# A convolution's very last half-image store as 120 partitions, with the other 8 in small pieces on one to seven DMA engines each

## The chip, the cores and the metric

One NeuronCore of a Trainium2 chip runs the whole program. The metric is device time of one execution in microseconds, the median of several executions, lower is better. A difference of under 2% counts as "same". TensorE, VectorE, ScalarE and GpSimd compute; SyncE issues the stores; 16 DMA engines move the data.

## The reference

A 3x3 convolution with padding 1 over 16 images of 64 channels and 64x64 pixels, to 128 output channels, in float32. Nine tenths of the weights are zero, but the kernel computes densely.

```python
batch, c_in, h, w, c_out, k = 16, 64, 64, 64, 128, 3
x_pad = np.pad(x, ((0, 0), (0, 0), (pad, pad), (pad, pad)))
# for every b, co, ci, kh, kw with weight != 0:
output[b, co] += weight[co, ci, kh, kw] * x_pad[b, ci, kh:kh+h, kw:kw+w]
```

One output image is 128 channels (partitions) x 64 rows x 64 columns x 4 bytes, 2 MB. All 16 are 33.55 MB.

## The kernel before

Images are computed in pairs. Each finished image is stored with one DMA; for the last pair the store is cut into two halves of 32 rows, so that less is left when compute ends. This loop is all that the change touches:

```python
    for p in range(NP):
        o = [o_pool.tile([C_OUT, H, W], FP32, name="o") for _ in range(2)]
        last = p == NP - 1
        for blk in range(4):
            r0 = 16 * blk
            # ... compute 16 rows of both images into o[0], o[1] ...
            if last and blk % 2 == 1:
                for n in range(2):
                    rows = slice(r0 - 16, r0 + 16)
                    nc.sync.dma_start(out=out[2 * p + n][:, rows, :], in_=o[n][:, rows, :])
        if not last:
            for n in range(2):
                nc.sync.dma_start(out=out[2 * p + n], in_=o[n])
```

The framework gives each DMA issued by SyncE one of eight completion semaphores, in rotation. A store that gets a semaphore first waits until that semaphore's previous user has landed. This is not visible in the code above.

## Time and profile before

| | kernel before |
|---|---|
| median (three runs) | 127.65 us |
| span of the profiled execution | 125.4 us |
| end of compute | 111.76 us |
| last packet of 15 DMA engines / of the sixteenth | 122.48 / 123.74 us |
| last arrival at the last store's semaphore | 124.20 us |

A store counts as landed when all its DMA engines have each added one to its semaphore; I call these additions **arrivals**. A 128-partition store has 16. The arrivals and the DMA packets are in the trace's own records, and tables of them are shown here in plain fences. The four half-image stores were issued by SyncE as follows (duration of an issue: smallest, median, largest):

```profile
L185 SPq DMA_DIRECT2D out_dram<-o x4: 332/417/612, 104.7 to 111.8; - x4
...
DMA to landing us min/median/max: 10.6/12.3/14.0
```

An issue takes a third to two thirds of a microsecond, and the data land ten or more later: there is a queue.

### The profile page before, as it was taken

The numbers are of one execution on the slowest core, as the hardware profiler recorded it, in microseconds if no ns is written. First come the engines' busy times: TensorE is split into PE (matmuls) and PEld (weight loads), VectorE is DVE, ScalarE is ACT, GpSimd is POOL, SyncE is SP. The second block draws the span as 40 slices with busy tenths as digits, with TensorE's granted clock in tenths as the row PEclk, the third lists the DMA queues.
The fourth block names the chain that finished last, engine by engine and source line by source line (L and its number), as shares of the span: only waits on it lengthen the run. The fifth ranks groups of instructions, "written<-read, shape, count | busy, mean of one in ns | idle before, by whom it ended". The sixth has DMA issues, their size and how long they took to land.

```text
span 125.4 us, 2486 instructions
## 1 busy us (share of the span) xinstructions
PE 107.5 (86%) x1002; PEld 58.8 (47%) x1002; DVE 82.4 (66%) x135; ACT 39.0 (31%) x71; POOL 40.7 (32%) x45
## 2 busy tenths in 40 slices
PE   6679999999999999999999999999999999920000
PEld 6435555555555555555555555555555555500000
DVE  0463877877787778777877787778777877760000
ACT  4555323333333333333333333333333333300000
POOL 6936533333333333333333333333333300000000
PEclk9999999999999999999999999999999999997555
DMA  5999999989999999999999999999999999999980
GB/s 146 338 222 220 212 214 220 191 259 350 324 311 337 308 293 319 342 316 308 426 429 423 408 429 434 450 416 434 418 418 429 429 444 423 434 397 423 423 369 10
DMA packets 4044, 42.93 MB, mean 342 GB/s; under 512 B 448, under 2 KB 448, under 8 KB 704
## 3 DMA queue, kind: packets, MB, share of 16 engines
q1 hardware_dynamic: 2880, 34.90, 66.2%
q0 software_dynamic: 1152, 7.86, 30.7%
q8 instruction: 8, 0.13, 0.4%
q14 instruction: 4, 0.03, 0.1%
HBM read 17.07 MB, written 33.55 MB: 404 GB/s over the span
## 4 chain that ended last, share of the span: by engine, by line
PE 81%; DMA 4%; DVE 1%; issue 1%; DVEq 0%; SPq 0%
PE ps L135 81%; DMA o<-in_x_dram 4%; DVE o L168 1%; DVEq L214 0%; DVE x L87 0%; SPq L60 0%; DVEq L168 0%
## 5 line engine op out<-in xcount | busy, mean ns | idle before, releaser
L168 DVE TENSOR_TENSOR o<-ps,pc 128x512 f32<-128x512 f32 x124 | 77.8, 686 | 22.1 <-PE ps L135 19.8
L135 PE MATMUL ps<-x,wT 64*128 64x504 bf16 (+3 forms) x780 | 88.8, 373 | 1.5 <-DVE x L87 1.5
L135 PEld LDWEIGHTS <-wT 64*128 64x128 bf16 x966 | 55.2, 94 | 49.4 <-issue 1.5
L154 POOL TENSOR_TENSOR s<-x 128x512 bf16<-128x512 bf16 x31 | 35.6, 1152 | 57.7 <-PE ps L135 41.5
L161 ACT COPY pc<-ps 128x512 f32<-128x512 f32 x62 | 33.3, 589 | 64.0 <-issue 61.8
L135 PE MATMUL ps<-s,wT 64*128 64x512 bf16 (+1 forms) x186 | 25.7, 377 | 0.0
L74 PE MATMUL ps<-idle_rhs 128*128 128x128 bf16 x27 | 3.1, 310 | 1.0 <-DVE idle_rhs L71 1.0
L67 POOL DMA_DIRECT2D x<-in_x_dram x7 | 3.7, 561 | 0.0
L74 PEld LDWEIGHTS <-idle_rhs 128*128 128x128 bf16 x27 | 2.8, 144 | 1.0 <-DVE idle_rhs L71 1.0
L91 DVE CAST w_bf<-w_sb 128x192 bf16<-128x192 f32 (+1 forms) x4 | 1.3, 382 | 3.0 <-DMA w_sb<-in_weight_dram 3.0
L149 DVE COPY o<-ps 128x512 f32<-128x512 f32 x2 | 1.4, 692 | 2.0 <-PE ps L135 2.0
L148 ACT COPY o<-ps 128x512 f32<-128x512 f32 x2 | 1.2, 586 | 2.4 <-PE ps L135 2.4
L87 ACT CAST x<-o 128x576 bf16<-128x576 f32 (+1 forms) x2 | 1.5, 802 | 0.5 <-DMA o<-in_x_dram 0.5
L91 ACT ACT_TABLE_LOAD x1 | 1.3, 1283 | 0.7 <-PEq L203 0.7
L97 PE MATMUL ps<-ident,w_bf 128*128 128x128 bf16 x9 | 1.1, 292 | 0.4 <-DVE w_bf L91 0.4
L87 DVE CAST x<-o 128x576 bf16<-128x576 f32 x1 | 0.5, 460 | 1.4 <-DMA o<-in_x_dram 1.4
L91 ACT CAST w_bf<-w_sb 128x64 bf16<-128x64 f32 (+1 forms) x2 | 0.7, 418 | 1.9 <-DMA w_sb<-in_weight_dram 1.9
L97 PEld LDWEIGHTS <-w_bf 128*128 128x128 bf16 x9 | 0.8, 128 | 0.8 <-DVE w_bf L91 0.8
L101 DVE TENSOR_TENSOR wT<-ps,wT 128x384 bf16<-128x384 f32 x2 | 1.0, 550 | 0.0
L63 POOL DMA_DIRECT2D x<-in_x_dram x1 | 0.7, 696 | 0.8 <-POOLq L203 0.8
L71 DVE MEMSET idle_rhs<- 128x64 uint32 x1 | 0.1, 112 | 0.8 <-PEq L203 0.8
L110 ACT CAST wT<-ps 128x384 bf16<-128x384 f32 x1 | 0.5, 481 | 0.4 <-PE ps L97 0.4
(8 smaller groups left out, 1.9 us busy)
## 6 DMA issues: line engine op xcount, KB each, us to landing
out_dram<-o SPq DMA_DIRECT2D x14, 2048.0 KB, 19.8
x<-in_x_dram POOLq DMA_DIRECT2D x7, 1024.0 KB, 29.3
out_dram<-o SPq DMA_DIRECT2D x4, 1024.0 KB, 12.3
o<-in_x_dram SPq DMA_DIRECT2D x1, 1024.0 KB, 5.4
x<-in_x_dram POOLq DMA_DIRECT2D x1, 512.0 KB, 7.5
w_sb<-in_weight_dram SPq DMA_DIRECT2D x1, 288.0 KB, 3.1
```

The source lines that it names most:

```text
L67: nc.gpsimd.dma_start(out=xs[p], in_=pair(p))
L74: nc.tensor.matmul(idle_ps, idle_rhs, idle_rhs, start=True, stop=True)
L87: copy(out=xs[0][:, a:b, :], in_=x_head[:, a:b, :])
L91: copy(out=w_bf4[:, g, a:b, :], in_=w_v[:, k : k + b - a, :])
L97: nc.tensor.matmul(wps[:, j, :], src, ident, start=True, stop=True)
L101: nc.vector.tensor_tensor(out=wT[:, g], in0=wps, in1=wT[:, G1], op=SUB)
L135: nc.tensor.matmul(ps[n][:, lo:hi, c_lo:c_hi], tap(g, kw, n), src[q, a:b:step, c_lo + kw - 1 : c_hi + kw - 1], start=(i == 0), stop=(i == ...
L148: nc.scalar.copy(out=o[0][:, r0 : r0 + rows, :], in_=ps[0])
L149: nc.vector.tensor_copy(out=o[1][:, r0 : r0 + rows, :], in_=ps[1])
L154: nc.gpsimd.tensor_tensor(out=s, in0=xs[p][:, r0 : r0 + 16 : 2, :], in1=xs[p][:, r0 + 1 : r0 + 16 : 2, :], op=ADD)
L161: nc.scalar.copy(out=c, in_=shared[n])
L168: nc.vector.tensor_tensor(out=o[n][:, first : r0 + 16 : 2, :], in0=ps[n], in1=pc[n], op=ADD)
```

## The change

The idea is that a whole DMA engine is spared in the last store. A copy of 120 partitions uses 15 engines, so the sixteenth has nothing more to do after the third half-store. The missing 8 partitions are stored as small pieces of 1, 7, 2, 6, 3, 5, 4 and 4 partitions by 8 rows, which run on as many engines as they have partitions, in a staircase over engines 0 to 6. If the spared engine were the one that is always last, the end would come earlier.

```diff
                 for n in range(2):
-                    rows = slice(r0 - 16, r0 + 16)
-                    nc.sync.dma_start(out=out[2 * p + n][:, rows, :], in_=o[n][:, rows, :])
+                    pieces = [(0, 128, r0 - 16, r0 + 16)]
+                    if (blk, n) == (3, 1):
+                        pieces = [(0, 120, r0 - 16, r0 + 16)]
+                        for i in range(4):
+                            r = r0 - 16 + 8 * i
+                            pieces += [(120, 121 + i, r, r + 8), (121 + i, 128, r, r + 8)]
+                    for c0, c1, a, b in pieces:
+                        nc.sync.dma_start(
+                            out=out[2 * p + n][c0:c1, a:b, :], in_=o[n][c0:c1, a:b, :]
+                        )
```

## The prediction

> **What bounds the kernel now.** I read the page's slices first, for the engines busy at the end, then the chain of waits, then the DMA issues with SyncE's own waits, and last the tail in short stretches.
>
> The 40 slices (3.13 us each):
>
> ```profile
> PE   6679999999999999999999999999999999920000
> DVE  0463877877787778777877787778777877760000
> ...
> DMA  5999999989999999999999999999999999999980
> ```
>
> TensorE and VectorE are done in slice 36 (about 112 us), while the DMA engines stay full for three more slices. So the last 13 us are a queue of stores being emptied; compute does not set the end.
>
> The chain that ended last says something else:
>
> ```profile
> PE 81%; DMA 4%; DVE 1%; issue 1%; DVEq 0%; SPq 0%
> ```
>
> These shares add up to 87 to 88%. In order of time, the chain's last piece is an addition that ends at 111.76 us; the view does not follow the stores after it. The remaining 13.6 us are therefore read elsewhere, here the DMA issues (count, size, median time to landing) and SyncE's waits:
>
> ```profile
> out_dram<-o SPq DMA_DIRECT2D x14, 2048.0 KB, 19.8
> out_dram<-o SPq DMA_DIRECT2D x4, 1024.0 KB, 12.3
> ```
>
> ```profile
> SPq L214 <- DMA out_dram<-o: 11.6, 4, 4.4
> ```
>
> A half-image store needs 12.3 us to land although its packets need far less: it queues behind earlier stores. At the end SyncE waits 11.6 us for the last four of them. The tail in stretches (PE alone; the columns after PE are granted clock, DMA share, GB/s):
>
> ```profile
> 121.50:122.00 0.50, 0.00 (x0) 0.50 0.70 295
> 122.00:122.50 0.50, 0.00 (x0) 0.50 0.16 66
> ```
>
> ```profile
> 122.50:123.70 1.20, 0.00 (x0) 0.00 (x0) 0.00 (x0) 0.00 (x0) 0.00 (x0) 0.50 0.06 27
> ```
>
> From 122.5 to 123.7 us the DMA share is 0.06, which is 1/16: one engine alone still has packets. The packet records of the trace say the same: 15 engines end their last packet between 120.93 and 122.48 us, one ends at 123.74. In the semaphore records the last store's 16 arrivals run from 121.28 to 122.84, with the sixteenth at 124.20. That engine, **the straggler**, is 1.36 us late. Its lag grew during compute: from 62.5 to 110.9 us one engine's 16 KB packets took 634 to 662 ns, where the others took 611; after 112 us all 8 KB packets take 309 ns. From the last arrival to the end of the span is 125.36 - 124.20 = 1.16 us of closing barrier.
>
> **What the Trainium skill says.** All four places are in the page "DMA: Bandwidth & Descriptors".
> - "Why a DMA increments its semaphore by 16 and not by 1": the number of DMA engines of a copy is the largest one up to 16 that divides the slowest dimension, and SyncE's copies use the lowest-numbered ones. So 120 partitions use engines 0 to 14, and the pieces of 7, 2, 6, 3, 5, 4, 4 partitions use as many engines from 0 up. The trace before has only 128-partition copies, with 16 arrivals each; it does not test the rest.
> - "Latency and other measured facts": engines 7 and 15 are usually slower. The trace agrees that one engine is, but does not number its packets. The page's guess is contention from GpSimd-issued transfers; here the slow packets come after the last of those (landed at 62.78), so the guess does not fit.
> - "Queues, rings and completion order": one engine takes its descriptors in ring order, and the semaphore increment lands only after that engine's earlier writes. So pieces queued behind the 120-partition store do not delay its arrivals.
> - "Anatomy of one DMA": about 2.0 us fixed per copy, mostly the write's confirmation. The trace differs in size: the weight load is issued at 0.74 and has its first packet at 1.75 (1.01 us), and a last semaphore packet lands 0.31 (weight load) to 0.46 us (straggler) later.
>
> **The change part by part.**
> 1. Removed: the 16th engine's share of the last store, 8 packets x 309 ns = 2.47 us. If engine 15 is the straggler, it now ends at 123.74 - 2.47 = 121.27, below the second-latest engine at 122.48.
> 2. Added: 32 rows of 2 KB on engines 0 to 6, namely 8, 7, 6, 5, 3, 2, 1. A 2304-byte packet of the weight load took 93 ns, so 2 KB is about 83 ns (estimate); engine 0 gets 8 x (83 + 9 for the semaphore packet) = 0.74 us. Without further waits the end would lie between the old second-latest 122.48 and 122.48 + 0.74: a gain of 0.5 to 1.3 us. That is the intent, at most 1%.
> 3. Added: eight issues on SyncE. The four last stores' issue records last 332 to 612 ns; eight such are 2.7 to 4.9 us after 112.4, against a backlog lasting until 122. Hidden.
> 4. **Moved into the path: semaphores.** The order of SyncE's instructions, built from the changed kernel, shows the stores rotating over eight completion semaphores, each new store waiting for that semaphore's previous user. With nine stores in place of one, the last rotation is short. Previous users by the trace of before: pieces 1, 2, 3: landed 99.16, 104.30, 109.45, no wait. Piece 4: landed 114.42. Piece 5: 116.87. Piece 6: 119.32. Piece 7: the third half-store, 121.77. **Piece 8 waits for the 120-partition store itself.** The first seven waits end under the backlog. The eighth cannot: it starts a full small-DMA latency after the end of the very transfer that used to be the end.
>
> Sum, straggler = engine 15: the 120-partition store lands on engines 0 to 14 at 122.84, the old second-latest arrival. Then 0.05 (wait to issue, a guess) + 1.01 (issue to first packet) + 0.15 (a 2 KB packet starting on an idle engine; the weight load's first ones took 91 to 346 ns) + 0.01 (semaphore packet) + 0.40 (to landing) = 1.62, so 124.46. With 1.16 for the barrier the span is 125.62, against 125.36: +0.26 us. The gain of 1.36 us and the new serial step of 1.62 us nearly cancel. On the timed median: 127.65 + 0.26 = 127.91; I say 127.9.
>
> **The rivals.**
> - The wait doesn't bite, and the straggler's relief is kept: 0.5 to 1.3 us gained, 126.4 to 127.1. For it: the backlog hides everything up to piece 7. Against: piece 8's wait is in the built order, and its target is the last large transfer. I give it 8%.
> - The straggler is among engines 0 to 14. Then nothing is relieved, piece 8 starts after 124.20, and 1.62 us come on top: 129.3. For it: the page names 7 as well, and no record numbers the engine. Against: the change is built around leaving out the last one. 20%.
> - Issue to first packet is longer than at the start. For it: the first output store was issued at 21.60 and its first packet ran at 25.76, 4.2 us later, though beside a queue of loads. Against: at 122.9 us the engines are idle and the queue has been running. If it took 2 us more, 129.9; 6%.
> - The timed runs had a larger lag than the profiled one (127.12 us against 127.65): a straggler later by 0.5 us would be relieved by that much more, giving about 127.4, as long as piece 7, which still waits for engine 15, is issued in time.
>
> **Range and chances.** The main case gives 127.5 to 128.4, from 0.3 us either way in the latency terms and 0.5 us in the lag. The rival with another straggler pulls the upper end to 129.4; the rival with no wait is left mostly outside. Range 127.1 to 129.4. Faster by 2% would need -2.55 us, and the whole relief is 1.36: 0.01. Slower by 2% needs +2.55, which only the long issue latency or several unlucky terms together reach: 0.04.
>
> **What would show it right or wrong.** In SyncE's records of the changed kernel the issues of pieces 4 to 7 should stand at about 114.4, 116.9, 119.3 and 121.8, and the eighth right after the last arrival of the 120-partition store, near 122.9. That store should have 15 arrivals ending near 122.84; if they end near 124.2, the straggler is not engine 15. The tail should have a gap of about 1 us with next to no packets, then four 2 KB packets, and the span should end about 1.6 + 1.2 us after that store's last arrival. If the eighth issue stands before 118 us, my reading of the semaphores is wrong and the gain should be there. If compute ends at another time than 111.8 us, something else moved.

## The result, and the profile after

The changed kernel takes 129.42 us (129.37 to 129.81, four runs), the kernel before on the same occasion 127.69. The ratio is 1.0139, with a 95% interval of 1.0116 to 1.0162. The kernel is clearly slower, and 129.42 lies just above the predicted range.

SyncE's own waits in the changed kernel:

```profile
SPq L192 <- DMA out_dram<-o: 2.6, 2, 2.2
SPq L223 <- DMA out_dram<-o: 0.7, 1, 0.7
```

Line 192 is the store loop: pieces now wait for other stores' landing, which no half-image store before had to do noticeably. The final wait for the stores (line 223) is down to 0.7 us from 11.6, because SyncE spends that time issuing and waiting inside the loop. Its issues:

```profile
L192 SPq DMA_DIRECT2D out_dram<-o x12: 252/1007/2078, 106.5 to 125.1; - x12
```

The last of them stands at 125.1 us, 11.5 us after the end of compute. The tail in stretches (granted clock, DMA share and GB/s are the last three columns):

```profile
123.80:124.60 0.80, 0.00 (x0) 0.50 0.05 20
125.00:125.70 0.70, 0.00 (x0) 0.50 0.00 0
125.80:126.20 0.40, 0.00 (x0) 0.50 0.07 21
126.20:127.60 1.40, 0.00 (x0) 0.50 0.00 0
```

Around 124 us one engine works alone, as before. Then nothing moves, and from 125.80 the four packets of the eighth piece follow. The arrivals (us) show what each step waited for:

```
store                issue    arrivals, last ones          late ones
third half-store     112.99   ... 120.86 121.09            122.54
120 partitions       113.59   ... 123.57 123.62            125.05
1 partition          114.75   121.79                       -
7 partitions         115.86   ... 123.58 123.67            125.24
2 partitions         116.91   122.15 123.75                -
6 partitions         118.00   ... 123.50 123.92            125.42
3 partitions         120.13   122.87 123.06 124.09         -
5 partitions         121.81   ... 123.69 124.27            125.61
4 partitions         122.56   123.74 123.85 123.95 124.44  -
4 partitions         125.06   126.26 126.28 126.37 126.45  -
```

Each piece has as many arrivals with its data as it has partitions (seven for the piece of 7; one more update at the end of the issue is left out here), which fits one engine per partition. Two readings. First, the eighth piece is issued within 0.02 us of the 120-partition store's last arrival, and lands 1.40 us after that arrival. Second, **the late engine was not spared**. One of the 15 engines of the 120-partition store is 1.43 us behind the next. The pieces of 7, 6 and 5 partitions have a late arrival, and those of 1, 2, 3 and 4 have none. The late engine is therefore the fifth in the order in which copies fill the engines, number 4 if they fill from number 0 up, as the prediction reads the Trainium skill; the records do not number the engines. The change gives it three pieces on top of its full share.

The two profiled executions should not be subtracted as they are. In the first, compute ended at 111.76 us, here at 113.56. The reason is at the start, in the granted clock of the 40 slices, before and after:

```profile
PEclk9999999999999999999999999999999999997555
```

```profile
PEclk9968999999999999999999999999999999997555
```

In the changed kernel's execution the clock was at half for 3.4 us near 7 to 11 us. A second trace of the unchanged kernel (below) has the same dip, ends compute at 113.61, and is the one to compare with.

### The profile page after: what moved, and what is told of

Read it like the earlier page. It is cut to its first block, busy times and chain, and to the rows that moved or that the text cites. A ratio compares the mean times of both kernels' runs of the same rounds, so it can differ in the third digit from the quotient of the medians.

```text
span 127.6 us, 2494 instructions
## 1 busy us (share of the span) xinstructions
PE 108.5 (85%) x1002; PEld 56.1 (44%) x1002; DVE 82.3 (64%) x135; ACT 39.0 (31%) x71; POOL 40.8 (32%) x45
## 4 chain that ended last, share of the span: by engine, by line
PE 81%; DMA 4%; DVE 1%; issue 1%; DVEq 0%; SPq 0%
PE ps L135 81%; DMA o<-in_x_dram 4%; DVE o L168 1%; DVEq L223 0%; DVE x L87 0%; SPq L60 0%; DVEq L168 0%
## 5 line engine op out<-in xcount | busy, mean ns | idle before, releaser
L135 PE MATMUL ps<-x,wT 64*128 64x504 bf16 (+3 forms) x780 | 90.1, 378 | 2.2 <-DVE x L87 2.2
L135 PEld LDWEIGHTS <-wT 64*128 64x128 bf16 x966 | 52.9, 95 | 53.9 <-issue 3.9
L112 DVE CAST wT<-ps 128x384 bf16<-128x384 f32 x1 | 0.6, 551 | 0.0
```

The costliest lines, as they stand in the source:

```text
L135: nc.tensor.matmul(ps[n][:, lo:hi, c_lo:c_hi], tap(g, kw, n), src[q, a:b:step, c_lo + kw - 1 : c_hi + kw - 1], start=(i == 0), stop=(i == ...
```

## The experiments

All give correct results. A median is over all runs of that kernel. Bands of expected times that were missed are discussed below for a_seven, d_seven and h_seven. Missed as well: d_eight (129.20 for 128.6 to 129.0), h_eight (129.67 for 128.8 to 129.3), e_k5 (129.01 for 128.3 to 128.7), i_spread (128.05 for 127.2 to 127.6), e_k4_again (128.16 for 127.4 to 127.7), and, 0.1 us below their bands, e_k4 and f_two.

| label | last store | median us | ratio to before | interval |
|---|---|---|---|---|
| (changed kernel) | 120, then 1 7 2 6 3 5 4 4 | 129.42 | 1.0139 | 1.0116 to 1.0162 |
| after_again | the same again | 129.54 | 1.0132 | 1.0086 to 1.0179 |
| before_again | 128 | 127.71 | 0.9993 | 0.9956 to 1.0030 |
| a_seven | 120, then 1 7 2 6 3 5 8 | 128.89 | 1.0090 | 1.0058 to 1.0121 |
| g_merge | 120, then 8 2 6 3 5 4 4 | 128.71 | 1.0082 | 1.0049 to 1.0114 |
| b_one | 120, then 8 (all 32 rows) | 128.19 | 1.0034 | 1.0006 to 1.0062 |
| d_eight | 128 x 28 rows, then 8 pieces of 16 | 129.20 | 1.0123 | 1.0103 to 1.0143 |
| d_seven | 128 x 28 rows, then 6 of 16, one of 32 | 129.07 | 1.0115 | 1.0090 to 1.0141 |
| f_two | 128 x 28 rows, 128 x 4 rows | 127.61 | 0.9980 | 0.9948 to 1.0011 |
| h_eight | 112, then 8 pieces of 4 | 129.67 | 1.0153 | 1.0119 to 1.0188 |
| h_seven | 112, then 7 pieces of 4 | 128.47 | 1.0047 | 1.0012 to 1.0082 |
| e_k4 | 112, then 4 pieces of 4 | 127.52 | 0.9975 | 0.9946 to 1.0003 |
| e_k4_again | the same again | 128.16 | 1.0008 | 0.9945 to 1.0071 |
| i_spread | 112, then 4 of 4, partitions 4 apart | 128.05 | 1.0001 | 0.9952 to 1.0051 |
| e_k5 | 112, then 5 5 5 1 | 129.01 | 1.0095 | 1.0053 to 1.0137 |
| e_k5b | the same again | 129.12 | 1.0055 | 1.0011 to 1.0098 |

**The theory at the start**: the eighth piece's wait is what makes the change slower, and the relief is missing because the late engine is number 4. **The rival**: the small pieces cost by themselves, by their number or by SyncE's issue time of about 1 us each. The first round gave the rival a share that the theory had not allowed for.

### a_seven: no piece waits for the large store

```diff
-for i in range(4):
+for i in range(3):
     ...
+pieces += [(120, 128, r0 + 8, r0 + 16)]
```

> The change with the last two pieces (4 partitions each, 8 rows) merged into one of 8 partitions, so that seven pieces follow and no one waits for the 120-partition store. In the changed kernel's trace the last arrival of that store is at 125.05 us, piece 8 is issued at 125.06 and lands at 126.45. Theory (the eighth piece's wait is the cost, and the late DMA engine is the fifth, number 4, which gets pieces of 7, 6, 5 and now 8 partitions behind its share): the last arrival moves from 126.45 to about 125.7, so 128.6 to 128.8 us, still slower than before (127.7), and no gap near the end. Rival (the small pieces themselves cost, by their number or by about 1 us of issue each on SyncE): 129.2 to 129.4, since only one of nine issues is gone.

Measured 128.89 us, ratio 1.0090, 0.5% below the changed kernel and a little above the expected band. The trace says why the gain was smaller. The late engine's share of the 120-partition store arrives at 125.29, and its arrivals for the pieces of 7, 6, 5 and 8 follow at 125.48, 125.67, 125.86 and 126.04: **0.19 us apart**. Their 2 KB packets take 84 ns and the semaphore packets 9, and the engine's last packet had ended at 125.27. So each copy costs an engine about twice what its packets take. I had counted 0.09 per piece. Merging the last two pieces took the wait away and put a fourth piece on the late engine.

### b_one: one piece in place of eight

```diff
+pieces = [(0, 120, r0 - 16, r0 + 16), (120, 128, r0 - 16, r0 + 16)]
```

> The 120-partition store and all of the remaining 8 partitions as one second store on eight engines. Theory: no wait at the end; the late engine, number 4, gets one 8 KB packet more than before (0.31 us) and suffers the slower packets of the 120-partition store (about 0.3 us): 128.1 to 128.4 us. If the late engine were number 15, it would be relieved of 2.47 us here, and the time would be 126.6 to 127.4. Slow 8 KB packets (400 to 700 ns) while the 120-partition store runs are expected again if they come from its partition layout; none if they come from the 2 KB pieces.

Measured 128.19 us, ratio 1.0034, as the theory says. This is the experiment on the change's basic idea: no small pieces, no wait, and still no gain. If the spared engine had been the late one, 126.6 to 127.4 us was expected. Its 120-partition store still has a late arrival (124.89, the one before it 123.80), and so has the piece of 8 (125.19, the one before it 124.10).

The packets of the 120-partition store are slowed here too, without any 2 KB piece. Between 119 and 121 us, first this kernel, then the unchanged one (before_again):

```profile
119.00:121.00 2.00, 0.00 (x0) 0.50 0.97 381
```

```profile
119.00:121.00 2.00, 0.00 (x0) 0.50 1.02 430
```

The engines are 5% less busy and move 11% less. Added up from the end of compute on, 8 KB packets took 5.1 us of engine time more than 309 ns each would, 6.1 in the changed kernel and 0.006 in before_again. The sum differs much between traces with a 120-partition store: 2.0 in g_merge, 15.9 in after_again.

### d_eight and d_seven: the wait without uneven pieces

```diff
+pieces = [(0, 128, r0 - 16, r0 + 12)]
+pieces += [(16 * i, 16 * i + 16, r0 + 12, r0 + 16) for i in range(8)]   # d_eight
+# d_seven: range(6), then (96, 128, r0 + 12, r0 + 16)
```

> No 120-partition store and no uneven pieces: the last store is 128 partitions of 28 rows, then the last 4 rows as eight pieces of 16 partitions, all on 16 engines. The eighth piece waits for the 128-partition store. Theory (the wait is the cost): that store lands about 0.3 us earlier than in the kernel before, piece 8 is issued right after and lands 1.4 us later: about 128.6 to 129.0 us, 1.0 to 1.3 above its twin with seven pieces. Rival (number of pieces or their size): equal to the twin within 0.2.

> The twin: the same 28 rows, then six pieces of 16 partitions and one of 32, so no piece waits for the 28-row store. Theory: 127.6 to 127.9 us, as the kernel before within 0.2, with 309 ns packets throughout the 28-row store. Rival (small pieces cost by themselves): 128.5 or more.

They came out equal, 129.20 and 129.07 us, and d_seven missed its band by more than a microsecond: on this pair the rival won. The late engine's arrivals in d_seven:

```
28-row store 124.67; pieces 124.87 125.06 125.24 125.43 125.61 125.80 125.98
```

The engine's last packet ended at 124.56. After that it moved nothing, as this stretch of d_seven shows, and seven completions were still handed over 0.19 us apart:

```profile
124.60:126.00 1.40, 0.00 (x0) 0.50 0.00 0
```

In d_eight the eighth piece is issued at 124.80; fifteen of its arrivals are in by 126.22, and the last, 126.28, follows the late engine's arrival for the seventh piece (126.09) by 0.19. So the pair does not measure the wait, as I had planned it to: seven completions in a row (1.31 us) hide nearly all of a serial small store (1.42 us from its issue to the fifteenth arrival). The theory needed a second term, **0.19 us per copy on the late engine**, and a cleaner pair.

### f_two: the same bytes in two copies

```diff
+pieces = [(0, 128, r0 - 16, r0 + 12), (0, 128, r0 + 12, r0 + 16)]
```

> The last store as 28 rows and 4 rows, both of 128 partitions: the same bytes per engine as the seven-piece kernel on all 16 engines, with one more completion on each engine in place of seven. Theory (completions of successive copies on one engine arrive no closer than about 0.19 us, so that seven pieces cost 7 x 0.19 = 1.3): 0.2 us above the kernel before, 127.7 to 128.1, and 1.0 to 1.3 below that kernel (129.07). If splitting off the last 4 rows were the cost: 128.9 or more.

Measured 127.61 us, ratio 0.9980: not slower than before at all. Against d_seven that is 1.35% in the ratios, some 1.7 us, for the same bytes on the same engines with one extra copy in place of seven. It is more than expected, but the runs were on two chips, and the two traces differ by 1.32 us in the last arrival (124.66 and 125.98). Cutting this store in two cost nothing that the runs show; many completions on the engine that ends last do cost.

### g_merge: the changed kernel without its eighth piece

```diff
-pieces: 1, 7 (rows 0 to 8), 2, 6, 3, 5, 4, 4
+pieces: 8 (rows 0 to 8), 2, 6, 3, 5, 4, 4
```

> As the change, but the first two pieces (1 and 7 partitions of the same rows) are one of 8, so there are seven pieces, the late engine still gets three of them (8, 6 and 5 partitions, as it got 7, 6 and 5), and the last piece waits for the third half-store, not for the 120-partition store. Theory: in the changed kernel the late engine's last piece arrived at 125.61 us and the eighth piece at 126.45; only the second falls away, so 0.84 us less than the changed kernel: 128.4 to 128.7 us. Rival (the wait is incidental, small pieces cost by number): 129.2 to 129.3.

Measured 128.71 us, ratio 1.0082, against 1.0139: 0.57%, 0.7 us (against after_again's 1.0132 the intervals overlap). The late engine still gets three pieces, and its last arrivals are 124.53, then 124.72, 124.91 and 125.09 (the pieces of 8, 6 and 5; those of 2, 3 and 4 end by 123.73). The span ends 1.35 us after the last of them. Its profiled execution was one without the clock dip, so the comparison rests on the timed runs and on the distance to its own large store: 0.56 us here, 1.40 us in the changed kernel.

### h_seven and h_eight: the wait alone, off the late engine

```diff
+pieces = [(0, 112, r0 - 16, r0 + 16)]
+pieces += [(112 + 4 * i, 116 + 4 * i, r, r + 16) for i in range(4) for r in (r0 - 16, r0)]  # h_eight
+# h_seven: the last two of these are one piece of 32 rows
```

> The last store as 112 partitions (seven on each engine), the other 16 partitions in seven pieces of 4 partitions, which use engines 0 to 3 only; no piece waits for the 112-partition store. Theory (the late engine is number 4): it loses one 8 KB packet (0.31 us) and gets no piece, engines 0 to 3 get four packets' worth and finish just before it: about as the kernel before or 0.2 us better, 127.4 to 127.9 us. If the late engine is one of 0 to 3: 4 packets minus 1 plus seven completions on it, 129 or more. If small pieces cost in themselves wherever they run: 128.9 or more, as the seven-piece twin on all 16 engines did (129.07).

> The same with the seventh piece cut in two: the eighth piece now waits for the 112-partition store. Nothing else differs, and no piece is on the late engine, so the wait is measured alone this time. Theory: the eighth piece is issued when the late engine's share lands and arrives 1.4 us later: 1.2 to 1.5 us above the seven-piece twin, 128.8 to 129.3 us. If waiting costs nothing: equal to the twin within 0.2.

No piece touches engine 4 here, and the pair differs in one cut. The difference is 1.06% in the ratios, 1.35 us (1.20 in the medians), within the expected 1.2 to 1.5. The tail of h_seven, then of h_eight:

```profile
124.90:126.50 1.60, 0.00 (x0) 0.50 0.00 0
```

```profile
124.40:125.40 1.00, 0.00 (x0) 0.50 0.00 0
125.40:126.20 0.80, 0.00 (x0) 0.50 0.11 20
```

In h_eight the 112-partition store's last arrival is 124.74, the eighth piece is issued at 124.76, nothing moves for more than 0.7 us, and the piece lands at 126.47. So **the wait costs 1.2 to 1.4 us by itself** where nothing else hides it.

h_seven alone missed its band (128.47 for 127.4 to 127.9). Its seventh piece waits for the third half-store, whose last arrival was 122.97 in that trace, and took until 125.34 to land, just after the late engine (125.24). Its four engines read four neighbouring partitions, 8 KB each, and their packets took 856 to 1044 ns. In h_eight the four 4 KB packets of the isolated last piece took 225 to 401 ns for 159 alone, 0.64 us from first to last, which is 4 x 159. The Trainium skill's page "SBUF — State Buffer", section "Door 1: The DMA port swizzle", says that four neighbouring partitions share one port; this piece behaves so.

### e_k4 and e_k5: pieces that stop short of engine 4, and pieces that reach it

```diff
+pieces = [(0, 112, r0 - 16, r0 + 16)]
+pieces += [(112 + 4 * i, 116 + 4 * i, r0 - 16, r0 + 16) for i in range(4)]           # e_k4
+pieces += [(112, 117, ...), (117, 122, ...), (122, 127, ...), (127, 128, ...)]        # e_k5
```

> 112 partitions, then four pieces of 4 partitions, which reach engines 0 to 3 alone; as many pieces as the kernel with pieces of 5, run again beside it. Late engine number 4: it has seven packets for eight and no further completion, but the 112-partition store's slower packets (0.3 to 0.5 us): 127.6 to 128.1 us, and 0.7 to 1.2 us below the twin with pieces of 5. Late engine above 4: both equal.

> 112 partitions, then three pieces of 5 partitions and one of 1: pieces reach engine 4 as well as 0 to 3, with 8 KB packets, and none waits. Theory (late engine number 4): it has 7 + 3 packets in place of 8 and three more completions: 0.6 to 0.8 us above the kernel before and 0.7 to 1.1 above the seven-piece kernel on engines 0 to 3: 128.3 to 128.7 us. If the late engine has a number above 4: as h_seven, 127.4 to 127.9.

> The pieces of 5 partitions once more, because its trace fell on an execution with late compute and its times spread over 1.6 us. Late engine number 4: the sixteenth arrival of the 112-partition store is followed by late arrivals in all three pieces of 5 and not in the piece of 1; 128.5 to 129.2 us. Otherwise as its twin.

e_k4 has a ratio of 0.9975 and e_k5b of 1.0055, 0.8% or 1.0 us apart; the expectation was 0.7 to 1.2. In e_k4's trace the late engine arrives at 124.48 and the pieces of 4 by 124.30. The two traces of e_k5 do not show what was expected of them. In both, all five arrivals of the first piece of 5 (by 126.18; in e_k5b by 127.98) come before the last arrival of the 112-partition store (126.57; 128.05), so the late engine there is none of numbers 0 to 4 (if one engine's arrivals come in order of issue, as those 0.19 us apart did), and in e_k5 the piece of 1 lands last of all (126.99). Both fell on executions in which compute ended late (117.22 and 118.81 us). The record shows where that began: the last arrival of the first input load came 2.42 and 4.53 us after its fifteenth, for 0.01 in the kernel before; why is open. In both the store queue ran dry after 100 us, and the lag of one engine, 1.16 us before that in e_k5, was 0.05 at the next store. So "engine 4" is read from executions in which the lag had built up without a break. Whether the timed runs of e_k5 were late in the same way is not known, so the pair is weak support; the evidence is in the arrivals of the other kernels.

### before_again and after_again: second traces

No edit.

> The kernel before, unchanged, for a second trace of it. Its first trace was of an execution of 127.12 us, half a microsecond faster than its timed median. If that execution was merely early, this one ends compute near 113.5 us as the others do, and its last store's sixteenth arrival stands near 124.7 us, some 1.3 us after the fifteenth. If the later arrivals in the changed kernel came from the change, it stands at 124.2 again. The time equals the kernel before.

> The changed kernel again, for a second trace: the sixteenth (fifteenth counted) arrival of the 120-partition store some 1.4 us after the one before, late arrivals in the pieces of 7, 6 and 5 partitions and not in those of 1, 2, 3 and 4 (late engine number 4), the eighth piece issued within 0.05 us of that arrival and landing 1.4 us later: 129.2 to 129.7 us. If the late engine changes from execution to execution or from chip to chip, another set of pieces is late.

before_again ends compute at 113.61 and has its last arrival at 124.84, 1.56 us after the fifteenth; its span is 125.98. The clock between 7 and 12 us (third column from the end), first trace, then second:

```profile
7.00:12.00 5.00, 4.88 (x46) 2.60 (x47) 2.85 (x6) 2.52 (x5) 3.36 (x3) 1.00 1.07 222
```

```profile
7.00:12.00 5.00, 4.71 (x30) 2.25 (x31) 2.32 (x5) 1.87 (x3) 3.36 (x3) 0.66 1.07 223
```

With the dip TensorE got 30 matmuls done there in place of 46. Compute ends 1.85 us later, but the last arrival only 0.64 us later: the store queue absorbs the rest.

after_again confirms the reading in a second execution, on chip 6 (the record does not name the first one's): 129.54 us. The 120-partition store's last arrival is 125.73 (the one before 124.78, a lag of 0.95 where 1.4 was expected); the late arrivals are 125.92, 126.11 and 126.30, in the pieces of 7, 6 and 5, while those of 1 to 4 end by 125.39; the eighth piece is issued at 125.75 and lands at 127.14.

### i_spread and e_k4_again: is there a version that beats both?

```diff
-[112 + 4 * i : 116 + 4 * i]
+[112 + i : 128 : 4]
```

> The best kernel so far (112 partitions, then four pieces of 4 partitions), with each piece of 4 taken from partitions 4 apart instead of neighbours. If engines that read neighbouring partitions share one port of the on-chip memory, the neighbours cost up to four times 309 ns a packet when nothing else runs and the spread ones 309 ns; the late engine takes no piece, so the time moves little: 127.2 to 127.6 us, at or up to 0.3 below the twin. If ports have nothing to do with it, the packets of the pieces look alike in both.

> The twin with neighbouring partitions, again, on the same chip as its spread form and the changed kernel: 127.4 to 127.7 us and 0.1 to 0.5 per cent below the kernel before, if relieving the late engine of one packet of 0.31 us is real; equal to it otherwise.

Ratios of 1.0001 and 1.0008, with intervals that hold 1: e_k4's 0.9975 was not confirmed, and **no version beats the kernel before**. The test of ports was inconclusive: in both kernels nearly all packets of the pieces took 309 ns, probably because the four engines reach the pieces at different times and seldom meet. What slows the packets of the 120-partition store is therefore not settled. The partition layout goes with it: from the end of compute on, the traces with 120 or 112 partitions in the last large store have 1.2 to 15.9 us of extra engine time in 8 KB packets, those with 128 at most 0.14. It is not the only cause, as in e_k5's trace five 8 KB packets took 429 to 716 ns between 115.0 and 117.2 us, before the 112-partition store was issued. That it is port sharing is not shown.

## Why the prediction was wrong

The measured 129.42 us is 0.02 us above the range and 1.5 us above the point. Like for like (before_again against the changed kernel, both with the clock dip):

| | unchanged | changed | difference |
|---|---|---|---|
| compute ends | 113.61 | 113.56 | -0.05 |
| third half-store, last arrival | 122.41 | 122.54 | +0.13 |
| last large store, last arrival | 124.84 | 125.05 | +0.21 |
| eighth piece, last arrival | - | 126.45 | +1.40 |
| closing barrier | 1.14 | 1.15 | +0.01 |
| span | 125.98 | 127.60 | +1.62 |

- **What bounds the kernel**: right. Compute ends at the same time in both, and the drain of the stores and its one late engine set the end.
- **Part 1, the removed share: the step that failed.** The prediction said "If engine 15 is the straggler, it now ends at 123.74 - 2.47 = 121.27" and built its sum on it, a gain of 1.36 us. The late engine is number 4, in the arrivals of the changed kernel, after_again, a_seven and g_merge, and b_one shows in time that sparing the sixteenth engine brings nothing. In place of -1.36 the term is +0.21: the late engine keeps its full share, and some 8 KB packets are slower from the moment the 120-partition store runs. Why one engine is late, and why that one, stays open.
- **Part 2, the added pieces**: the packet estimate was good (84 ns measured, 83 estimated). The price per piece was not: 0.19 us on an engine, not 0.09, because completions are handed over no faster. In the changed kernel this is hidden under the wait (the late engine's pieces are through at 125.61, before 126.45); it is part of what keeps g_merge and a_seven slow, whose last pieces land 0.56 and 0.75 us after the late engine's share of the large store.
- **Part 3, SyncE's issues**: hidden, as predicted, but longer: 7.7 us in total for 2.7 to 4.9. Five of the eight took 1.0 to 2.1 us each, so pieces 4 to 7 were issued at 118.0, 120.1, 121.8 and 122.6, not at the predicted 114.4 to 121.8, and only the seventh and the eighth had a semaphore left to wait for (the two waits of 2.6 us in SyncE's view).
- **Part 4, the semaphores**: right in kind and nearly in size. The eighth piece waits for the large store and is issued 0.02 us after its last arrival. The serial step was estimated at 1.62 us and measured at 1.40: 0.74 from issue to first packet (1.01 expected), 0.32 of packets, 0.33 to the last arrival. g_merge and h_eight against h_seven show it alone.
- **The rivals**: the one called "The straggler is among engines 0 to 14" came true. Its figure, 129.3, is the result within 0.1 us, in part by luck: its step of 1.62 us measured 1.40, and the 0.21 by which the large store lands later was not in it. I gave it 20% and set the upper end of the range at 129.4. The evidence for engine 15 was the shape of the change and one line on a page, none of it from a trace; a step on which 1.6 us hang deserved more doubt.
- **What would show it**: the test named in the prediction ("if they end near 124.2, the straggler is not engine 15") is what gave the answer. The expected 124.2 was itself 0.6 us early (124.84 in before_again), because the profiled execution was one without the clock dip.

## What to carry to other kernels

Before relieving "the slow DMA engine", find out which one it is, in more than one execution: a few copies with rising partition counts at the end show it by which of them land late. Small copies after a large one are not free even when their bytes are: here each costs the engine about 0.19 us for its completion, and a framework that rotates a few completion semaphores may make the last copy wait for the large one, 1.4 us here, where nothing was left to hide it. Of the cuts of the last store tried here none beat the single 128-partition store.

## What the Trainium skill lacked or had wrong

- "DMA: Bandwidth & Descriptors", section "Latency and other measured facts": engines 7 and 15 are given as usually slower, with GpSimd-issued transfers as the guess. Here it is number 4 (counted as that page's section "Why a DMA increments its semaphore by 16 and not by 1" fills them) in four traces, on chips 6, 7 and 13 and one not recorded; in two others (e_k5, e_k5b), where the store queue had run dry, it is none of 0 to 4. In the kernel before, one engine's 16 KB packets took 634 to 662 ns for 611 long after the last GpSimd-issued transfer.
- The same page, section "Anatomy of one DMA — SWDGE (gpsimd) path", calls the semaphore write on trn2 essentially free, and no page has a spacing of completions. In the runs, for copies that SyncE issued, completions of successive copies on the late engine come no closer than 0.18 to 0.19 us, while a 1 KB packet and its semaphore packet take 55 ns together: seven pieces cost 1.31 us after the data were through (d_seven).
- The same section's fixed cost of about 2.0 us is for copies that GpSimd issues; the page has no such fit for SyncE's. Here a 4-partition store took 1.40 us on idle engines, 0.32 of it packets, and a 16-partition one 1.42 us to its fifteenth arrival (d_eight).
- The same page, section on the number of engines: it does not say which partitions each engine gets when SyncE's copy uses fewer than 16, nor that a copy of fewer than 128 partitions can have slower packets. From the end of compute on, 8 KB packets took 2.0 to 15.9 us of engine time more than 309 ns each in the five traces with a 120-partition store, and at most 0.14 in those where all large stores had 128.
- No page says how long an issue takes SyncE while many copies are queued: 1.0 to 2.1 us in the changed kernel for pieces whose semaphores were long free, where the first issue of the kernel before took 0.38 us.
